# Six of eight merge_b column tiles moved into the attention stage, and the gate weights' loads moved to GpSimd's queue

## The chip, the cores and the metric

The kernel runs on one core of a Trainium2 chip. The metric is device time in microseconds: from the first to the last instruction of the program, with what lies around it. Several executions of the same kernel are taken, and the median is what counts. Beside them one execution was taken with the hardware profiler; all rows below are from that one.

## The reference, cut to what matters

Two blocks of a network run one after the other on 512 tokens of width 1024 in float32. The part that is changed is the end of the first block. `h` is the normalised input, `proj = h @ w_in`, and `merge` is the last 2048 columns of it:

```
m_a, m_b = jnp.split(merge, 2, axis=-1)
y = (jax.nn.sigmoid(m_a) * y_a + jax.nn.sigmoid(m_b) * y_b) @ w_out[l]
x = x + gate[:, None, :] * rms_norm(y, g_post[l])
```

`y_a` and `y_b` are the outputs of two attentions (compressed, selected and windowed heads; sliding-window heads with sinks), each multiplied by `silu(z)` and by its own output matrix. `gate` is a third of `c @ w_ada + b_ada`, so it needs the last 1024 columns of `w_ada` and the vector `c`, but not `h`. The second block (a short convolution mixer and an mLSTM mixer) is not touched.

## The kernel before, in words

All activations lie transposed: a tile has 128 of the 1024 columns on its partitions and the 512 tokens along the free dimension. Float32 products are made of three fast matmuls: both operands are split into a high and a low part (`mm3`, line 481), and `proj` (line 489) adds up eight such triples, 24 matmuls of 512 columns, for one column tile.

**Weights.** All weights are cut into units of 128 x 1024 and used in one fixed order, the list `units` (lines 445 to 474). `Weights` (line 372) has SP load a unit into one of three staging tiles; ScalarE casts the high part `whi`, VectorE subtracts to get the low part `wlo`, into one of three pairs of parts. `W.get()` gives the next unit and starts splits and loads ahead.

**Order.** Every engine call is noted in a `Plan` (line 191) with a duration, a latency and a priority, which is its place in program order. `flush` (line 315) runs a list scheduler over the operations noted since the last flush and emits them: on each engine, of the operations that are ready by its own clock, the one with the smallest priority number. What it emits is each engine's fixed order on the chip. While `plan.prio` is `FILL` (1e6) an operation is taken only when nothing else of its engine is ready. A load issued by GpSimd is priced at 1.0 us for the issue, one issued by SP at 0.05 us (line 207), and either one's data at 345 GB/s (line 357).

**The attention stage** (lines 854 to 1037). Its filling work are sixteen column tiles (lines 886 to 895): eight tiles of `zt`, the `z` gates with silu applied, and eight tiles tanh(m_a / 2), kept in `ma`, a view of `x1`. They go through PSUM banks 6 and 7 in turn. The attention itself is a list of 32 steps: four blocks of 128 queries in the order 1, 2, 3, 0 (`ORDER`), in each two groups of heads and four kinds (`KINDS`). `scores` makes the scores (banks 0 and 1), VectorE adds distances and takes the minimum, ScalarE the exponentials, GpSimd scales the rows; `pv_step` transposes them (banks 2 and 3) and multiplies them with the values (banks 4 and 5). At the end of a group the result is multiplied into the columns of this query block in `zt`; after the second group these columns are split into a high part (ScalarE) and a low part (GpSimd) in `QS` (lines 1030 to 1032). From then on these columns of `zt` are not read any more.

**The merge stage** (lines 1058 to 1103) takes column tiles in four pairs. For each pair there are 48 matmuls on `QS` with a unit of `woa` and one of `wob` (`pab`, four tiles), and 48 on `h` with two units of `wmb`, whose tanh is kept in `tb`. Then VectorE and ScalarE form `(1 + ma) * y_a + (1 + tb) * y_b` and split it into `Th` and `Tl`. Also in each pair `gate_cols` (line 1063) loads 1 MB of `wada` into the only buffer `ada2` and multiplies it by `c` on VectorE, nine operations into `mg`; `gate_mm` sums over the partitions with four tiny matmuls. The loads go through SP's queue, between the loads of the units. `y` (line 1108) then takes the product with `w_out`, in a tile of its own.

**Pools.** A tile pool closes at the end of its phase, and what comes into its memory later waits for all of it.

Of the kernel before, what the change touches and what calls it, by code (L numbers as in the profile page):

```python
# [10 lines left out]
F32 = mybir.dt.float32  # L11
F32R = mybir.dt.float32r
AF = mybir.ActivationFunctionType
OP = mybir.AluOpType
PSUM = bass.MemoryType.PSUM

S = 512
D = 1024
KT = 8
# [6 lines left out]
ORDER = (1, 2, 3, 0)  # L26
KINDS = "swcb"
FILL = 1e6
HALF = T // 2


# [399 lines left out]
def trunk(ctx, tc, a, out):  # L431
    nc = tc.nc
    plan = Plan(nc)
    V, A, G, PE, SP = plan.dve, plan.act, plan.pool, plan.pe, plan.sp

    def pool(stack, name, space=None):
        return Pool(stack.enter_context(tc.tile_pool(name=name, bufs=1, **({"space": space} if space else {}))))

    @contextmanager
    def phase():  # L440
        with ExitStack() as stack:
            yield stack
            plan.flush()
# [3 lines left out]
    def add(name, n, w=1024):  # L447
        for i in (range(n) if isinstance(n, int) else n):
            units.append((a[name][i], w))
# [3 lines left out]
    for i in range(4):  # L453
        add("wm", [i])
        add("wc1", [2 * i, 2 * i + 1])
    add("wm", range(4, 23))
    for p in range(4):
        add("woa", [p])
        add("wob", [p])
        add("wmb", [2 * p, 2 * p + 1])  # L460
    add("wout", 8)
    add("wout", 8)
    for f in range(16):
# [14 lines left out]
    bank = Banks(pool(ctx, "psum", PSUM))  # L478
    W = Weights(plan, wpool, units, 3, 3)
# [6 lines left out]
    def kview(w, kt):  # L486
        return [t.rearrange("p (k c) -> p k c", k=kt) for t in w]

    def proj(ps, w, u, kt=KT, c=slice(0, 128)):

        for k in range(kt):
            mm3(ps, (w[0][:, k, c], w[1][:, k, c]), (u[0][:, k], u[1][:, k]), k == 0, k == kt - 1)
# [83 lines left out]
    hh, hl = uh[:, :, META:], ul[:, :, META:]  # L576
# [58 lines left out]
    with phase() as sx:  # L635
        sp = pool(sx, "sp")
# [56 lines left out]
        for h in (slice(0, 256), slice(256, 512)):  # L693
# [8 lines left out]
            if h.start:  # L702
                m = ada_mac(0)
# [10 lines left out]
        for k in range(KT):  # L714
# [3 lines left out]
            if k + 2 < KT:  # L718
                G.tensor_tensor(x1[:, k + 2, META:], x1[:, k + 2, META:], rbc, op=OP.mult)
                m = ada_mac(k + 2)  # L720
# [12 lines left out]
        among = (2, 3, 4, 5, 0, 1)  # L733
# [6 lines left out]
        t = big(F32)  # L740
# [3 lines left out]
        for q in range(4):  # L744
            wh, wl = kview([t[:, :816] for t in W.get()], 2)
            for t in range(4):
                for kk in range(2):
                    k = 2 * q + kk
# [102 lines left out]


    ma = x1[:, :, META:]
    with phase() as sx:
        sp = pool(sx, "sp2")
        zt = sp.tile([128, 8, S], F32, name="zt")
        B = sp.tile([128, 128 + S], F32, name="B")
        slp = sp.tile([128, 2, 8], F32, name="slp")
        base3 = sp.tile([128, 4, 32], F32, name="base3")
# [27 lines left out]
        for m in range(16):  # L887
            ps = bank(among=(6, 7))
# [102 lines left out]
        steps = []  # L991
# [6 lines left out]
        def pv_step(st, sc):  # L998
            i, g, t, first, last, both = st
            P, k0, nk = sc  # L1000
            if first:
                acc[t == "b"] = bank(among=(4, 5))
            o = acc[t == "b"]
            nj = (nk + 127) // 128
            n = min(nk, 128)
            prev = None
            for jj in range(nj + 1):
                cur = trans(P, jj * 128, n) if jj < nj else None
                if prev is not None:
                    jb = jj - 1  # L1010
                    if t == "c":
                        PE.matmul(o, vcs[:, g], prev[0][:96], start=False, stop=last)
                    else:
                        w = vv[:, k0 // 128 + jb, "swb".index(t), 2 * g:2 * g + 2].rearrange("p a d -> p (a d)")
                        for e in range(2):
                            PE.matmul(o, w, prev[e], start=first and jb == 0 and not e,
                                      stop=last and jb == nj - 1 and e == 1)
                prev = cur
            if last:
                p0 = 4 if t == "b" else 0  # L1020
                qb = slice(i * 128, i * 128 + 128)
                s = slice(64 * g, 64 * g + 64)
                out_g = zt[:, p0:p0 + 4, qb]

                av = sp.tile([128, S], F32, name="av", tag="P", bufs=10)
                A.copy(av[s], o[64 - 64 * g:128 - 64 * g])
                V.tensor_tensor(av[s], av[s], o[s], op=OP.add)
                V.tensor_tensor(out_g[s], av[s].rearrange("p (j q) -> p j q", j=4), out_g[s], op=OP.mult)
                if both:
                    hi = QS[:, p0:p0 + 4, 0, qb]  # L1030
                    A.copy(hi, out_g)
                    G.tensor_tensor(QS[:, p0:p0 + 4, 1, qb], out_g, hi.bitcast(F32), op=OP.subtract)

        for st in steps:
            pv_step(st, scores(*st[:3]))
        W.ahead = 2
    plan.flush()
    kvx.close()
# [19 lines left out]
    with phase() as sx:  # L1058
        sp = pool(sx, "sp3")
# [2 lines left out]

        def gate_cols(i):
            t = sp.tile([128, KT, 256], F32, name="ada2", tag="ada2", bufs=1)
            SP.dma_start(t, a["wada"][8 + i].rearrange("p (k c) -> p k c", k=KT))
            m = [sp.tile([128, 256], F32, name=f"mg{e}", tag=f"mg{e}", bufs=2) for e in range(2)]
            for e in range(2):
                V.tensor_scalar(m[e], t[:, e], vec[:, V_C + e:V_C + e + 1], 0.0, op0=OP.mult, op1=OP.add)
            for k in range(2, KT):
                V.scalar_tensor_tensor(m[k % 2], t[:, k], vec[:, V_C + k:V_C + k + 1], m[k % 2], op0=OP.mult, op1=OP.add)  # L1070
            V.tensor_tensor(m[0], m[0], m[1], op=OP.add)
            return m[0]
# [9 lines left out]
        for p in range(4):  # L1082
            pab = []
            for q0 in (0, 4):
                w = kview(W.get(), 4)
                for e in range(2):
                    ps = bank()
                    proj(ps, w, (QS[:, q0:q0 + 4, 0], QS[:, q0:q0 + 4, 1]), 4, slice(e * 128, e * 128 + 128))
                    pab.append(ps)
            m = gate_cols(p)  # L1090
            for e in range(2):
                pm = bank()
                proj(pm, kview(W.get(), KT), (hh, hl))
                mi = 2 * p + e
                tb = sp.tile([128, S], F32, name="tb", tag="tb", bufs=2)
                ua = sp.tile([128, S], F32, name="ua", tag="ua", bufs=2)
                A.activation(tb, pm, AF.Tanh, scale=0.5)
                V.scalar_tensor_tensor(ua, ma[:, mi], 1.0, pab[e], op0=OP.add, op1=OP.mult)
                V.scalar_tensor_tensor(tb, tb, 1.0, pab[2 + e], op0=OP.add, op1=OP.mult)
                V.tensor_tensor(ua, ua, tb, op=OP.add)  # L1100
                A.activation(Th[:, mi], ua, AF.Copy, scale=0.5)
                V.scalar_tensor_tensor(Tl[:, mi], ua, 0.5, Th[:, mi].bitcast(F32), op0=OP.mult, op1=OP.subtract)
            gate_mm(p, m)
# [1 line left out]
            for k in range(0, KT, 4):  # L1105
                SP.dma_start(x1[:, k:k + 4, META + h:META + h + 256], a["xT"][h // 256, :, k:k + 4])
        SP.dma_start(x1[:, :, :META], a["metaT"].rearrange("(k p) t -> p k t", p=128))
        y = sp.tile([128, KT, S], F32, name="y")

        def wout_half(hf, between):  # L1110
            rs = RS[hf]
# [67 lines left out]
                proj(conv_ps[q][e], conv_w[q], (uh[:, :, HS[e]], ul[:, :, HS[e]]))  # L1179
        W.split_to(W.used + 1)  # L1180


    with phase() as sx:
        sp = pool(sx, "sp4")
# [583 lines left out]
```

## Time and profile before

| | us |
|---|---|
| median of 3 runs | 1512.63 |
| lowest and highest run | 1509.63, 1514.08 |
| the profiled execution: its own time | 1511.26 |
| its span, first to last instruction | 1509.2 |

In the rows further below, PE is TensorE's matmuls and PEld its weight loads, DVE is VectorE, ACT ScalarE, POOL GpSimd and SP the sync engine; a name like SPq or DVEq is that engine's queue of instructions that do not count as busy. Times are microseconds from the start of the span, or nanoseconds where a row gives the mean of one instruction. A matmul's duration in a row overlaps with that of the next: what one costs is read from the distance between two starts. PEclk is the granted clock of TensorE in a stretch, 1.00 being 2.4 GHz. Names after an arrow are what an instruction or a wait was waiting for. Since nearly all recorded operations have the line of the helper that emits them (L254), the tile names tell them apart: `uh` and `ul` are the parts of `h`, `qs` those of the gated attention, `whi` and `wlo` those of a weight unit, `mg` and `ada` the gate product and its weights.

### The profile page before, as it was taken

What the parts mean: (1) busy time and instruction counts of PE and PEld (TensorE: products, weight loads), DVE (VectorE), ACT (ScalarE), POOL (GpSimd) and SP (SyncE); (2) the same over time, 40 slices, a digit from 0 to 9 for tenths busy, and PEclk for the clock granted to TensorE, in tenths of its full rate; (3) what the DMA queues carried; (4) which work ended last, traced back from release to release, by engine and by line L of the source; (5) the groups of instructions that cost most, each with busy time, mean ns of one, the idle gap of its engine ahead of it and who ended that gap; (6) DMA issues with size and microseconds to landing.
All of it is one profiled execution on the core that took longest, in us unless ns stands there. A gap on an engine that the chain in (4) does not pass through costs nothing.

```text
span 1509.2 us, 22556 instructions
## 1 busy us (share of the span) xinstructions
PE 1463.2 (97%) x8965; PEld 1300.1 (86%) x8965; DVE 880.3 (58%) x1710; ACT 606.4 (40%) x1103; POOL 248.2 (16%) x292
## 2 busy tenths in 40 slices
PE   5999999988999899999999999999999999999997
PEld 5787888856889899999999999988888888887886
DVE  7976758776558754454544545755534635453465
ACT  3475757772247422122212122554333333433333
POOL 3210323440002210011001001302002101100201
PEclk8999999989999999999999999999999999999998
DMA  6544121005445232222222222221222222222221
GB/s 232 181 130 149 58 83 43 15 1 183 154 137 171 71 98 85 98 85 98 85 89 94 91 93 79 97 84 55 89 81 84 70 98 71 70 98 83 72 70 56
DMA packets 44121, 142.60 MB, mean 94 GB/s; under 512 B 5745, under 2 KB 12145, under 8 KB 42609
## 3 DMA queue, kind: packets, MB, share of 16 engines
q1 hardware_dynamic: 44016, 141.17, 28.3%
q8 instruction: 70, 1.15, 0.3%
q14 instruction: 35, 0.28, 0.1%
HBM read 139.06 MB, written 2.10 MB: 94 GB/s over the span
## 4 chain that ended last, share of the span: by engine, by line
PE 74%; DVE 2%; DMA 0%; issue 0%; ACT 0%; DVEq 0%; ACTq 0%
PE bank L254 74%; DVE ul L254 0%; DVE y L254 0%; DVE wlo L254 0%; DMA ada<-in_wada 0%; DVE so L254 0%; DVE num L254 0%; DVE x L254 0%; DVE mg L254 0%; DVE ss L254 0%; DVE nss L254 0%; DVEq L1764 0%; ACT Dm L254 0%; DVE tb L254 0%; DVE rb L254 0%
## 5 line engine op out<-in xcount | busy, mean ns | idle before, releaser
L254 PE MATMUL bank<-ul,whi 128*128 128x264 f32 (+1 forms) x1784 | 570.8, 324 | 2.7 <-DVE ul L254 2.5
L254 PE MATMUL bank<-uh,whi 128*128 128x264 f32 (+1 forms) x1784 | 570.6, 325 | 2.2 <-ACT uh L254 2.2
L254 PE MATMUL bank<-uh,wlo 128*128 128x264 f32 (+1 forms) x1768 | 565.9, 324 | 0.0
L254 ACT CAST whi<-wst 128x1024 fp32r<-128x1024 f32 (+2 forms) x236 | 244.6, 1038 | 621.2 <-PE bank L254 452.1
L254 DVE TENSOR_TENSOR wlo<-wst,whi 128x1024 fp32r<-128x1024 f32 (+1 forms) x227 | 279.3, 1232 | 193.8 <-ACT whi L254 192.4
L254 PEld LDWEIGHTS bank<-ul,whi 128*128 128x128 f32 x1784 | 335.8, 188 | 28.9 <-DVE ul L254 4.0
L254 PEld LDWEIGHTS bank<-uh,whi 128*128 128x128 f32 x1784 | 335.4, 189 | 28.6 <-ACT uh L254 3.9
L254 PEld LDWEIGHTS bank<-uh,wlo 128*128 128x128 f32 x1768 | 333.4, 189 | 24.8 <-DVE wlo L254 0.4
L254 DVE TENSOR_TENSOR zr<-bank,rb 128x264 f32<-128x264 f32 (+1 forms) x64 | 35.8, 559 | 118.9 <-PE bank L254 118.9
L254 DVE TENSOR_TENSOR x<-x,bank 128x264 f32<-128x264 f32 (+2 forms) x102 | 49.9, 496 | 68.9 <-PE bank L254 67.4
L254 POOL TENSOR_TENSOR yv<-yv,rb 128x528 f32<-128x528 f32 x16 | 22.7, 1419 | 335.1 <-DVE yv L254 316.8
L254 PE MATMUL bank<-gh,wlo 128*128 128x264 f32 x256 | 72.5, 284 | 0.0
L254 PE MATMUL bank<-gl,whi 128*128 128x264 f32 x256 | 72.4, 283 | 0.0
L254 PE MATMUL bank<-gh,whi 128*128 128x264 f32 x256 | 72.3, 284 | 0.0
L254 POOL TENSOR_SCALAR P<-P,sm 128x256 f32<-128x256 f32 (+3 forms) x96 | 49.7, 536 | 84.4 <-DVE sm L254 38.2
L254 PE MATMUL bank<-whi,uh 128*128 128x512 f32 (+1 forms) x160 | 61.7, 386 | 0.3 <-DVE ak L254 0.3
L254 PE MATMUL bank<-wlo,uh 128*128 128x512 f32 (+1 forms) x160 | 61.7, 386 | 0.0
L254 PE MATMUL bank<-whi,ul 128*128 128x512 f32 (+1 forms) x160 | 61.6, 385 | 0.0
L254 ACT ACTIVATE P<-P,nm 128x256 f32<-128x256 f32 (+3 forms) x96 | 50.8, 530 | 7.4 <-DVE nm L254 6.1
L254 PE MATMUL bank<-Gh,whi 128*128 128x512 f32 (+1 forms) x144 | 53.5, 371 | 0.0
L254 PE MATMUL bank<-Gl,whi 128*128 128x512 f32 (+1 forms) x144 | 53.3, 370 | 0.0
L254 PE MATMUL bank<-Gh,wlo 128*128 128x512 f32 (+1 forms) x144 | 53.3, 370 | 0.0
(336 smaller groups left out, 2294.2 us busy)
## 6 DMA issues: line engine op xcount, KB each, us to landing
wst<-in_wci SPq DMA_DIRECT2D x64, 512.0 KB, 3.4
wst<-in_wqkv SPq DMA_DIRECT2D x32, 512.0 KB, 3.4
wst<-in_wzo SPq DMA_DIRECT2D x32, 512.0 KB, 3.4
wst<-in_wm SPq DMA_DIRECT2D x23, 512.0 KB, 3.4
ada<-in_wada SPq DMA_DIRECT2D x11, 1024.0 KB, 5.2
wst<-in_wout SPq DMA_DIRECT2D x16, 512.0 KB, 4.1
wst<-in_wco SPq DMA_DIRECT2D x16, 512.0 KB, 3.5
wst<-in_wmo SPq DMA_DIRECT2D x16, 512.0 KB, 3.4
```

The costliest lines, as they stand in the source:

```text
L254: call(*[v.real() if isinstance(v, View) else v for v in args], **{k: v.real() if isinstance(v, View) else v for k, v in kw.items()})
```

## The change

Three column pairs' `wmb` units (six of eight) come before the merge's units in the list. After each of the first three query blocks (8, 16 and 24 steps) two of these tiles are noted with `FILL` priority, through banks 6 and 7, and their tanh is written into the 4 x 128 columns of `zt` which this query block has freed; `mb` keeps the views. In the merge these six tiles have no matmuls left, and the product reads `mb` in place of `tb`. `zt` lives on through the merge, in a pool on the right side of the memory, and `y` is written over it. The loads of `gate_cols` are issued by GpSimd. All pools get `reuse_waits="tile"`: a new tile waits for the tiles in whose memory it lies, not for their whole pool.

```diff
+N_EARLY = 6
...
-    def pool(stack, name, space=None):
-        return Pool(stack.enter_context(tc.tile_pool(name=name, bufs=1, **({"space": space} if space else {}))))
+    def pool(stack, name, space=None, **kw):
+        return Pool(stack.enter_context(tc.tile_pool(name=name, bufs=1, reuse_waits="tile", **({"space": space} if space else {}), **kw)))
...
     add("wm", range(4, 23))
+    add("wmb", N_EARLY)
     for p in range(4):
         add("woa", [p])
         add("wob", [p])
-        add("wmb", [2 * p, 2 * p + 1])
+        add("wmb", [m for m in (2 * p, 2 * p + 1) if m >= N_EARLY])
...
+    zx = ExitStack()
+    zt = pool(zx, "zp", side="right").tile([128, 8, S], F32, name="zt")
+    mb = []
     with phase() as sx:
         sp = pool(sx, "sp2")
-        zt = sp.tile([128, 8, S], F32, name="zt")
...
-        for st in steps:
+        for n, st in enumerate(steps):
             pv_step(st, scores(*st[:3]))
+            if (n + 1) % 8 == 0 and len(mb) < N_EARLY:
+
+                plan.prio = FILL
+                for e in range(2):
+                    ps = bank(among=(6, 7))
+                    proj(ps, kview(W.get(), KT), (hh, hl))
+                    mb.append(zt[:, 4 * e:4 * e + 4, st[0] * 128:st[0] * 128 + 128])
+                    A.activation(mb[-1], ps.rearrange("p (n c) -> p n c", n=4), AF.Tanh, scale=0.5)
+                plan.prio = 0
         W.ahead = 2
...
-            SP.dma_start(t, a["wada"][8 + i].rearrange("p (k c) -> p k c", k=KT))
+            G.dma_start(t, a["wada"][8 + i].rearrange("p (k c) -> p k c", k=KT))
...
             for e in range(2):
-                pm = bank()
-                proj(pm, kview(W.get(), KT), (hh, hl))
                 mi = 2 * p + e
...
-                A.activation(tb, pm, AF.Tanh, scale=0.5)
+                if mi >= N_EARLY:
+                    pm = bank()
+                    proj(pm, kview(W.get(), KT), (hh, hl))
+                    A.activation(tb, pm, AF.Tanh, scale=0.5)
...
-                V.scalar_tensor_tensor(tb, tb, 1.0, pab[2 + e], op0=OP.add, op1=OP.mult)
+                tbv, gate, o = tb, tb, pab[2 + e]
+                if mi < N_EARLY:
+                    tbv, o = (t.rearrange("p (n c) -> p n c", n=4) for t in (tb, o))
+                    gate = mb[mi]
+                V.scalar_tensor_tensor(tbv, gate, 1.0, o, op0=OP.add, op1=OP.mult)
...
-        y = sp.tile([128, KT, S], F32, name="y")
+        y = zt
...
+    zx.close()
```

## Rows read from the trace of the kernel before

**Rows 1.** The page, part 1: busy us, share of the span, instructions.

```profile
PE 1463.2 (97%) x8965; PEld 1300.1 (86%) x8965; DVE 880.3 (58%) x1710; ACT 606.4 (40%) x1103; POOL 248.2 (16%) x292
```

**Rows 2.** The chain that ended last: start us, us, what.

```profile
344.92 4.92 DMA ada<-in_wada
...
352.06 1.15 DVE wlo L254
...
510.23 984.01 PE bank L254 x6397
```

**Rows 3.** Windows: us, busy us of each engine, granted clock, DMA share, GB/s.

```profile
146.10:303.41 157.31, 155.68 (x819) 129.23 (x818) 117.66 (x370) 108.04 (x287) 50.99 (x97) 1.00 0.15 48
303.41:340.43 37.02, 30.43 (x139) 21.15 (x137) 30.33 (x127) 29.00 (x102) 15.44 (x38) 0.82 0.00 1
340.43:353.25 12.82, 9.04 (x27) 6.41 (x26) 5.46 (x13) 3.80 (x6) 2.96 (x2) 0.73 0.41 129
353.25:437.36 84.11, 84.11 (x374) 69.05 (x375) 49.63 (x83) 23.80 (x30) 0.00 (x0) 1.00 0.49 169
```

**Rows 4.** Timeline of TensorE: start us, us, what; four stretches at full clock.

```profile
301.39 0.60 PE L254 MATMUL bank<-ident,P 128*128 128x128 f32 x4
...
302.06 0.39 PE L254 MATMUL bank<-pl,vv 128*128 128x512 f32 x1
...
308.89 0.28 PE L254 MATMUL bank<-khw,qs 128*128 128x128 f32 x1
309.00 0.28 PE L254 MATMUL bank<-klw,qs 128*128 128x128 f32 x1
...
425.85 0.40 PE L254 MATMUL bank<-uh,whi 128*128 128x512 f32 x1
...
431.44 0.40 PE L254 MATMUL bank<-uh,whi 128*128 128x512 f32 x1
```

**Rows 5.** Groups of TensorE by shape, 303.4 to 353.24: busy us, mean ns, idle before.

```profile
L254 PE MATMUL bank<-ident,P 128*128 128x128 f32 x48 | 11.3, 325 | 1.7 <-POOL P L254 1.6
L254 PE MATMUL bank<-qs,whi 128*128 128x512 f32 x18 | 8.0, 526 | 2.0 <-ACT qs L254 1.5 <-POOL qs L254 0.6
L254 PE MATMUL bank<-pl,vv 128*128 128x512 f32 x14 | 7.5, 538 | 1.8 <-DVE pl L254 1.7
L254 PE MATMUL bank<-ph,vv 128*128 128x512 f32 x13 | 6.9, 531 | 1.3 <-ACT ph L254 0.9
L254 PE MATMUL bank<-qs,wlo 128*128 128x512 f32 x8 | 3.9, 482 | 0.0
L254 PE MATMUL bank<-ident,Pc 128*32 128x128 f32 x12 | 3.2, 370 | 0.0
L254 PE MATMUL bank<-khb,qs 128*128 128x128 f32 x8 | 2.8, 356 | 0.0
...
L254 PE MATMUL bank<-ph,vcs 96*128 96x512 f32 x3 | 1.8, 593 | 0.0
```

**Rows 6.** Groups by shape, 341.5 to 441: busy us, mean ns, idle before.

```profile
L254 DVE TENSOR_TENSOR wlo<-wst,whi 128x1024 fp32r<-128x1024 f32 x18 | 21.9, 1222 | 23.5 <-ACT whi L254 23.5
L254 ACT CAST whi<-wst 128x1024 fp32r<-128x1024 f32 x18 | 18.8, 1048 | 49.1 <-PE bank L254 32.4 <-DMA wst<-in_wmb 8.1 <-DVE wlo L254 4.5
...
L254 DVE SCALAR_TENSOR_TENSOR mg<-ada,vec,mg 128x256 f32<-128x256 f32 x24 | 10.7, 481 | 0.1
L254 DVE TENSOR_TENSOR ua<-ua,tb 128x512 f32<-128x512 f32 x8 | 5.5, 689 | 0.2
...
L254 ACT ACTIVATE tb<-bank 128x512 f32<-128x512 f32 x8 | 4.7, 592 | 0.0
```

**Rows 7.** Timeline of GpSimd: the last low parts written from zt.

```profile
323.31 1.28 POOL L254 TENSOR_TENSOR qs<-zt,qs 128x512 fp32r<-128x512 f32 x1
...
341.94 2.96 POOL L254 TENSOR_TENSOR qs<-zt,qs 128x512 fp32r<-128x512 f32 x2 [5.52 <-ACT qs L254]
```

**Rows 8.** The tile ada: its thirteen loads on SP's queue, from issue to landing.

```profile
DMA to landing us min/median/max: 4.7/5.5/9.9
```

## The prediction

> **What bounds the kernel now.** I read the page first: TensorE is busy for 97% of the span, no other engine for more than 58% [rows 1]. So only two kinds of change can pay: less TensorE work, or fewer gaps between it. This one keeps every matmul and moves six tiles of them. The second view was the chain that ended last [rows 2]. From 510.23 us on it is one piece of TensorE work, 984 us long, so whatever is gained or lost before that point arrives at the end unchanged. Its first pieces are no matmuls: a transfer of gate weights, then VectorE. The third view, the windows [rows 3], says where the gaps are. While the attention has filling work (146.10 to 303.41) TensorE is busy 155.68 of 157.31 us. From 303.41, when the last filling matmul has been issued, to the attention's last matmul at 340.43, it is busy 30.43 of 37.02 us at a mean granted clock of 0.82, that is partly at the lower of its two levels, 1.2 instead of 2.4 GHz. To 353.25 the clock is 0.73 and 9.04 of 12.82 us are busy. From there to 437.36 the merge has no gap at all. The whole prize therefore lies between 303.41 and 353.25, and "busy" understates it, since a matmul at the low clock counts as busy for longer. I price those matmuls at full speed instead.
>
> **Price of that stretch at full speed.** A merge_b tile of 24 matmuls with 512 columns takes 431.44 - 425.85 = 5.59 us, 0.233 us each; a score matmul 0.11 us; four transposes and one 512-column matmul 0.67 us, so 0.44 us for four transposes [rows 4]. The stretch holds 30 matmuls of 512 columns on the values, 26 on qs, 6 x 8 score matmuls (one of the six alike forms is shown), and 48 + 12 transposes [rows 5]. The attention's own part is 30 x 0.233 + 48 x 0.11 + 15 x 0.44 = 18.9 us, the 26 of the merge are 6.1 us. Of 37.02 us the attention leaves 18.1 free; of the next 12.82, 6.7 are free. **Sum: 24.8 us can be won.**
>
> **The six tiles.** They remove 6 x 5.59 = 33.5 us of TensorE work from the merge and put as much into the attention, behind the sixteen tiles that are there (later count, same FILL priority). By the price above about 18.1 us, three tiles, fit into the attention's gaps; the other 15.4 us stand behind its last matmul and cover what TensorE waited for there: the last gated columns (VectorE, ScalarE, then GpSimd) and the low part of the second weights, held up behind the gate weights [rows 2]. 15.4 is more than 6.7, so 8.7 us remain as cover if the attention ends later. It will end a little later: each tile brings a cast of 1.05 and a tanh of 0.59 us on ScalarE and a split of 1.22 us on VectorE [rows 6]. For the three tiles in the gaps that is 4.9 and 3.7 us, against 29.00 and 30.33 us busy of 37.02 [rows 3]: both fit, tightly. For six it would be 9.8 and 7.3, and ScalarE would need 38.8 of 37.02. The planner gives these operations the lowest priority, so the attention's go first; the 8.7 us take the rest. The nearest row for how well filling works is the stretch before, which lost 1.6 of 157 us [rows 3]; the tail has thinner margins, so I take 2 us lost, between 0 and 18.1 (nothing fits).
>
> The destinations cost nothing in time: two tiles go into columns of a query block that is gated and split already. The last of the three blocks is read for the last time at 323.31 + 1.28 us [rows 7], and its tiles are the fifth and sixth, after 340 by the count above. Cover gone, a tanh that waits there would hold ScalarE's queue and with it the exponentials. The output y in zt waits for gates read a merge earlier: nothing. The pools' waits by tile instead of by pool could free a few first instructions of a phase sooner; inside 303 to 353 that is counted already, elsewhere I take 0, between 0 and 2 us.
>
> **The merge that is left.** Three column pairs now have only 48 matmuls, 11.2 us; the fourth keeps 96, 22.4 us. VectorE has per pair two splits (2.4), the gate product (eight operations of at most 0.48: 3.8), eight products of 0.69 (5.5, of which one form is shown) and 0.3 of small ones: 12.0 us, for the fourth 14.4 with its two more splits [rows 6]. VectorE thus becomes as long as TensorE in three pairs. It may fall behind by 8.7 us (TensorE still fills) plus 22.4 - 14.4 = 8.0 in the fourth pair, so three pairs may take it 33.6 + 16.7 = 50 us. Into that goes the wait for the gate weights, one buffer, so that each load starts when the product before is done. GpSimd's queue holds nothing else here (0.00 busy, [rows 3]), and SP's weight loads no longer stand behind a load that waits. The trace has no load issued by GpSimd. The nearest rows are SP's own: issue to landing 4.7 to 9.9 us, median 5.5 [rows 8]. The planner prices it at 1.0 + 3.04 = 4.0 us (lines 207 and 357) and puts the product into VectorE's order accordingly, so VectorE stands for what exceeds 4.0, and splits and gate products stand behind it. At 5.5 three pairs take 3 x 13.5 = 40.5 us, under 50: free. At 9.9 they take 53.7: 4 us lost. I take 2 us for uneven arrival, between 0 and 4.
>
> The Trainium skill, SBUF — State Buffer, section Who interferes with whom, speaks against the move: a DMA issued by GpSimd can starve while VectorE holds the port pair that they share. By the figure in its section on the bandwidth-pool intuition (620 to 3100 ns, five times) the landing would be some 27 us, an estimate, and the merge would lose 55 us. No run of before shows it; whether a slow landing hurts is worked out as a rival below.
>
> **Sum.** 24.8 - 2 - 2 = 20.8 us. The profiled execution took 1511.26 us, 1.4 under the median of the three runs: 1490.5 us against it, **1491.9 us** against the median.
>
> **Rivals.** *A, the gaps stay empty:* splits at the lowest priority come too late on crowded VectorE and ScalarE, and the tiles run behind the attention. Only the 6.7 us of waits go, less 2: 1507.9 us. For it speaks that VectorE is busy 82% of that stretch; against it the 155.68 of 157.31 us, with the same kind of filling and VectorE at 75% [rows 3]. *B, it does less than it says:* filling uses two PSUM banks, and a tile's bank is free only after its tanh. If the write into zt waits for more than its own columns (the last reads of zt begin at 341.94, [rows 7]), only two tiles, 11.2 us, fit into the gaps. 6.9 us more are lost: 1498.8 us. Nothing in the trace excludes that. *C, slower:* the load through GpSimd lands late, VectorE stands in its order, splits come late and TensorE waits. With landing L, three pairs take VectorE 3 x (8 + L) us; the gain of 22.8 us is used up at L = 16.3. At L = 20 it is 84 - 50 = 34 us lost: 1523.8 us. Against it: the longest landing shown is 9.9. *D, no change:* the extra work makes the attention end late by as much as is won: ScalarE and VectorE serve one chain, and 9.8 + 7.3 us in a row, beyond the cover of 8.7, with A's loss, leave about nothing: 1512 us.
>
> **Numbers.** Differences under 0.3%, 4.5 us, can't be told from no change here. The forecast has 0.55 (1486 to 1496: losses up to 6, or none and the boundaries' 2), B 0.16, A 0.12, D 0.08, C 0.09. A lies on the edge of 4.5 us, two thirds of it faster. Faster 0.55 + 0.16 + 0.08 + 0.03 for the upper half of D's spread = 0.82, same 0.09, slower 0.09. The range reaches from the forecast's low end past B to the near side of A: 1486 to 1505.
>
> **What would show it.** Filling matmuls (uh, ul against weights) after the attention's sixteen tiles, about three before its last matmul; granted clock near 1.00 all through that stretch; no TensorE wait for qs or for the second low part; the merge about 34 us shorter; VectorE's waits for ada of some 1 to 3 us each and no TensorE wait behind them; the first attention stretch and all after the merge as they were. Wrong: a clock of 0.8 in the tail (A or B), a landing over 16 us (C), an attention that ends over 9 us later (D).

## The result and the profile after

Taken together in the same comparison, the changed kernel has a median of 1490.6 us (four runs, 1488.94 to 1492.32), the kernel before 1513.36 us (1509.63 to 1516.5). The ratio is 0.9856, 95% interval 0.9839 to 0.9873: the change makes the kernel faster, by 1.3 to 1.6%, 22.8 us by the medians. The profiled execution took 1492.32 us with a span of 1490.3 us; that of before had a span of 1509.2, so the two profiles differ by 18.9 us.

The page of the changed kernel, part 1 (busy time, share of the span, instructions), answers to [rows 1]:

```profile
PE 1453.2 (98%) x8965; PEld 1296.9 (87%) x8965; DVE 881.8 (59%) x1710; ACT 605.7 (41%) x1103; POOL 251.5 (17%) x296
```

The number of matmuls is the same, 8965. What changed is their order, their idle time and their clock, and GpSimd has four more instructions, the loads.

The windows of the changed kernel, with the columns of [rows 3]: the attention to the end of its sixteenth old tile (its 384 filling matmuls, counted in the trace), the rest of the attention to its last matmul, from there to the first matmul of the merge, and the merge to the first matmul of the product with `w_out`:

```profile
147.36:306.04 158.68, 157.15 (x818) 130.08 (x818) 117.73 (x369) 108.11 (x284) 48.72 (x89) 0.99 0.16 54
306.04:349.82 43.78, 42.22 (x233) 33.74 (x232) 37.97 (x136) 35.66 (x114) 22.16 (x47) 1.00 0.16 50
349.82:361.63 11.81, 11.81 (x52) 9.58 (x51) 2.62 (x6) 3.25 (x5) 2.85 (x3) 1.00 0.43 138
361.63:418.14 56.51, 56.51 (x257) 46.74 (x255) 44.66 (x82) 16.99 (x21) 1.60 (x3) 1.00 0.57 196
```

The second row stands for 303.41 to 340.43 in [rows 3], where TensorE was busy 30.43 of 37.02 us at a clock of 0.82. Now it is busy 42.22 of 43.78 at 1.00. The third and fourth rows have no gap at all. VectorE is busy 44.66 of the 56.51 us of the merge; the prediction counted 3 x 12.0 + 14.4 = 50.4, some of which (the first splits) lies before.

The first row is not what it was: the same work takes 158.68 us, where it took 157.31 in [rows 3], and the clock is 0.99 and not 1.00. All of that lies in one place, where the granted clock falls for a moment:

```profile
260.00:275.00 15.00, 14.01 (x68) 11.55 (x67) 11.95 (x33) 11.54 (x27) 6.26 (x9) 0.89 0.11 37
```

The change is not the cause by itself. Six of the fourteen profiles have this fall, all with four or six tiles moved. But the first profile with four tiles has it (0.89) and the second, of the same program, does not (1.00), though just before it TensorE waits the same 0.7 and 0.3 us for VectorE in both. Nor have it the two runs that differ from the changed kernel only in the queue or in the pools' waits. With the fall the stretch takes 158.6 to 158.7 us, without it 157.1 to 157.3.

The timeline of TensorE in the changed kernel: the attention's last matmul, the filling right behind it, and the end of the filling.

```profile
349.82 0.40 PE L255 MATMUL bank<-pl,vv 128*128 128x512 f32 x1
350.06 0.40 PE L255 MATMUL bank<-ul,whi 128*128 128x512 f32 x1
...
361.40 0.39 PE L255 MATMUL bank<-uh,wlo 128*128 128x512 f32 x1
361.63 0.63 PE L255 MATMUL bank<-qs,whi 128*128 128x512 f32 x2
```

From 350.06 to 361.63 there are 11.57 us of filling, 2.07 tiles at 5.59 us each [rows 4]. So 3.93 of the six tiles ran inside the attention, and the rest covered the wait for the gated columns.

All that TensorE waited for from 147 to 420 us in the changed kernel (total, times, longest):

```profile
PE bank L255 <- DVE Pc L255: 1.2, 3, 0.7
PE bank L255 <- DVE sm L255: 0.9, 1, 0.9
PE bank L255 <- DVE pl L255: 0.6, 1, 0.6
PE bank L255 <- POOL P L255: 0.2, 1, 0.2
```

No wait for `qs` is left, and none for a low part, where [rows 2, 5] had both.

**The account.** The table gives stretches of the two spans, each between two matmuls that can be found in both traces.

| stretch, us | before | after | difference |
|---|---|---|---|
| span start to the attention's first matmul | 146.1 | 147.4 | +1.3 |
| to the attention's last matmul | 193.8 | 202.4 | +8.6 |
| to the first matmul with `w_out` | 97.4 | 68.3 | -29.1 |
| to the next block's first matmul on its gates (`gh`) | 174.8 | 176.1 | +1.3 |
| to the end | 897.0 | 896.0 | -1.0 |

The two middle rows give 20.5 us, where the prediction had 20.8. 3.93 tiles are 22.0 us of TensorE work. The attention took them in and became 8.6 longer. Of this about 1.4 is the fall of the clock, which lies before the gaps; behind the sixteenth old tile it became 7.3 longer (43.8 against 193.8 - 157.3 = 36.5), so 22.0 - 7.3 = 14.7 us of its gaps were filled. The stretch behind lost 22.0 of work and 7.1 of waits and low clock. The first row of the table is no effect of the change: over the fourteen profiles of this case it lies between 143.3 and 147.5 us, whatever the kernel.

### The profile page after: what moved, and what is told of

The parts are those of the page before. It is cut to its first block, busy times and chain, and to the rows that moved or that the text cites. A ratio compares the mean times of both kernels' runs of the same rounds, so it can differ in the third digit from the quotient of the medians.

```text
span 1490.3 us, 22552 instructions
## 1 busy us (share of the span) xinstructions
PE 1453.2 (98%) x8965; PEld 1296.9 (87%) x8965; DVE 881.8 (59%) x1710; ACT 605.7 (41%) x1103; POOL 251.5 (17%) x296
## 3 DMA queue, kind: packets, MB, share of 16 engines
q1 hardware_dynamic: 43440, 136.98, 27.7%
## 4 chain that ended last, share of the span: by engine, by line
PE 91%; DVE 6%; ACT 1%; DMA 1%; issue 0%; POOL 0%; SPq 0%; DVEq 0%; POOLq 0%; ACTq 0%
PE bank L255 91%; DVE mac L255 2%; DVE wlo L255 1%; DMA x<-in_xT 0%; DVE zt L255 0%; DVE ul L255 0%; DMA wst<-in_wm 0%; DVE P L255 0%; POOL P L255 0%; ACT whi L255 0%; ACT P L255 0%; DVE pl L255 0%; SPq L255 0%; DVE ak L255 0%; DVE so L255 0%
## 5 line engine op out<-in xcount | busy, mean ns | idle before, releaser
L255 PE MATMUL bank<-Gl,whi 128*128 128x512 f32 (+1 forms) x144 | 53.3, 370 | 0.0
L255 PE MATMUL bank<-Gh,wlo 128*128 128x512 f32 (+1 forms) x144 | 53.3, 370 | 0.0
```

The costliest lines, as they stand in the source:

```text
L255: call(*[v.real() if isinstance(v, View) else v for v in args], **{k: v.real() if isinstance(v, View) else v for k, v in kw.items()})
```

## The experiments

The first four runs change the number of moved tiles or the queue of the gate loads.

**No tile moved.**

```diff
-N_EARLY = 6
+N_EARLY = 0
```

> N_EARLY = 0: no merge_b tile is moved; zt's place, the gate loads through GpSimd's queue and the waits by tile stay. Theory (the gain is TensorE's idle time in the attention's tail, filled by moved tiles): 1510 to 1514 us, nearly as before, at most some 2 us for the splits no longer held up behind the gate weights. Rival 1 (a good part comes from the loads or from the waits by tile): 1500 us or less.

Measured: 1508.66 us, ratio 0.9965 (0.9951 to 0.998). It is 1.3 us below what was expected, and far from the rival. By the medians, what is left of the change without its tiles is worth some 4 us (5 by the ratio), and the tiles the other 18.

**Two tiles.**

```diff
-N_EARLY = 6
+N_EARLY = 2
```

> N_EARLY = 2: two tiles moved, 2 x 5.59 = 11.2 us of filling. Theory: the tail has 24.8 us to fill, so both tiles pay in full: 1500 to 1503 us. Rival 2 (every moved tile pays a sixth of the gain, 3.7 us): 1505 to 1507.

Measured: 1498.49 us, ratio 0.9904 (0.9881 to 0.9927). Both tiles pay in full, as the theory has it; the time is 1.5 us below its range, which did not count the some 4 us that the run before won without tiles. The attention (first to last matmul) is 194.6 us long, against 193.8 before: 11.2 us of work went in for 0.8 us of time. What TensorE waited for from 300 to 460 us in this run shows that the gaps behind the attention, the waits for `qs`, are still there:

```profile
PE bank L255 <- ACT ph L255: 1.8, 2, 1.5
PE bank L255 <- ACT qs L255: 1.5, 1, 1.5
PE bank L255 <- POOL qs L255: 1.1, 1, 1.1
```

**Four tiles.**

```diff
-N_EARLY = 6
+N_EARLY = 4
```

> N_EARLY = 4: 22.4 us of filling against 24.8 us of room. Theory: nearly all is won with four tiles; 1490 to 1494 us, as with six or up to 3 us above. Rival 2 (a sixth each): 1497 to 1500.

Measured: 1488.36 us, ratio 0.984 (0.9808 to 0.9873), below the expectation and at least as fast as six. All four tiles lie inside, but for two matmuls. The windows of this run, its attention behind the sixteenth old tile and its merge:

```profile
304.81:348.25 43.44, 42.00 (x234) 33.77 (x233) 36.74 (x135) 34.73 (x113) 21.21 (x47) 1.00 0.14 39
...
348.90:416.60 67.70, 67.70 (x306) 55.80 (x304) 48.24 (x89) 21.23 (x27) 3.58 (x5) 1.00 0.56 194
```

The merge begins 0.7 us after the attention's last matmul and has no gap, without the 11.57 us of filling that six tiles put there. The attention ends 202.1 us after its start, about as late as with six (202.4), but both have the fall of the clock at 260 to 275 us. Without it, in the later profile of this same program, it takes 200.5 us, and with six tiles 200.9. So the four tiles fill 22.4 - (200.5 - 193.8) = 15.7 us of gaps, 5.3 more than the first two alone (11.2 - 0.8 = 10.4). What the third and fourth bring besides is behind the attention: the waits for `qs` are gone, and the stretch from the last matmul to `w_out` falls from 83.8 us with two tiles to 68.3, which is 4.3 more than their own 11.2. The fifth and sixth fill nothing: with six the same stretch takes 68.3 too.

**Six tiles, the gate weights on the sync engine's queue as before.**

```diff
-            G.dma_start(t, a["wada"][8 + i].rearrange("p (k c) -> p k c", k=KT))
+            SP.dma_start(t, a["wada"][8 + i].rearrange("p (k c) -> p k c", k=KT))
```

> Six tiles moved, the gate loads back on SP's queue, waits by tile. Theory: the tiles alone make the gain and VectorE's slack in the merge covers a load from either queue: 1489 to 1493 us, as the change. Rival 3 (GpSimd's queue is needed: on SP the gate loads wait for the product and hold up the units' loads, now with half the TensorE work per pair): 1496 us or more, with TensorE waits in the merge.

Measured: 1490.77 us, ratio 0.9852 (0.9826 to 0.9878). The rival falls: with six tiles GpSimd's queue gives nothing. The first load leaves at 347.10 us, 0.4 after the attention's last matmul, and VectorE waits for the gates 2.2 us in two waits, as the rows for VectorE say:

```profile
DVE mg L255 <- DMA ada<-in_wada: 2.2, 2, 1.6
```

**Six tiles, waits for whole pools.**

```diff
-... bufs=1, reuse_waits="tile", **({"space": space} if space else {}), **kw)))
+... bufs=1, **({"space": space} if space else {}), **kw)))
```

> The changed kernel with waits for whole pools, as before, and all else kept. The prediction priced the waits by tile at 0 (0 to 2 us). Theory: they are worth about 1 us at the end of the program (last stage 14 to 15 us after the last matmul instead of 13.9), and at the start of the merge nothing, because filling matmuls run there: 1490 to 1493 us. Rival: without them the new pool on the right side and what lies in the attention's memory wait for everything of the phase before, at several boundaries: 1496 us or more, with TensorE idle at 361 to 365 us.

Measured: 1488.93 us, ratio 0.9851 (0.9836 to 0.9866). The time is 1.1 us below the expected range; its profile is one of those without the fall of the clock in the attention. Nothing is lost at the start of the merge, as expected. The microsecond at the end was not lost either (896.1 us from `gh` to the end, as in the changed kernel), so the waits by tile do not give it. With six tiles they are worth nothing that can be measured.

**Late gate loads.** This is the prediction's rival C, tried by making it true: each load is issued three times in a row, priced as one.

```diff
-            G.dma_start(t, a["wada"][8 + i].rearrange("p (k c) -> p k c", k=KT))
+            src = a["wada"][8 + i].rearrange("p (k c) -> p k c", k=KT)
+            plan.add("POOL", lambda: [nc.gpsimd.dma_start(t.real(), src) for _ in range(3)], [], [t], 1.0, 2.0, None, t.arr.size * 4)
```

> The changed kernel, but each of the four loads of gate weights is issued three times in a row by GpSimd, so that the data land late while the planner still prices one load. This tries the prediction's rival C. Theory: the landing takes 16 to 20 us instead of 5 to 7.5; VectorE stands in its fixed order for it, the splits behind it come late and TensorE waits. By the prediction's sum, three pairs take VectorE 3 x (8 + 18) = 78 us, of which 50 are free: some 28 us lost, 1510 to 1522 us. Rival: the loads run so far ahead of their product that the transfer stays hidden: under 1497 us and no TensorE wait for a low part.

Measured: 1521.19 us, ratio 1.0066 (1.005 to 1.0083), in the theory's range and slower than the kernel before. The timeline of GpSimd in this run shows the three issues of the first load (each waits until the one before has landed) and the first issue of each later one:

```profile
353.99 0.74 POOL L1079 DMA_DIRECT2D ada<-in_wada  x1
360.48 0.54 POOL L1079 DMA_DIRECT2D ada<-in_wada  x1 [5.74 <-DMA ada<-in_wada]
365.78 0.53 POOL L1079 DMA_DIRECT2D ada<-in_wada  x1 [4.76 <-DMA ada<-in_wada]
376.34 0.53 POOL L1079 DMA_DIRECT2D ada<-in_wada  x1 [10.03 <-DVE mg L255]
...
397.65 0.53 POOL L1079 DMA_DIRECT2D ada<-in_wada  x1 [8.31 <-DVE mg L255]
...
420.51 0.53 POOL L1079 DMA_DIRECT2D ada<-in_wada  x1 [7.91 <-DVE mg L255]
```

and the timeline of VectorE the start of the gate product with its wait:

```profile
370.78 0.62 DVE L255 TENSOR_SCALAR mg<-ada,vec 128x256 f32<-128x256 f32 x2 [17.85 <-DMA ada<-in_wada]
...
393.76 0.62 DVE L255 TENSOR_SCALAR mg<-ada,vec 128x256 f32<-128x256 f32 x2 [8.65 <-DMA ada<-in_wada]
...
417.23 0.62 DVE L255 TENSOR_SCALAR mg<-ada,vec 128x256 f32<-128x256 f32 x2 [12.27 <-DMA ada<-in_wada]
```

From the first issue to the product it is 16.8 us, then 17.4, and for the third load 19.6: 17.9 on average. TensorE's waits from 360 to 450 us show the rest of the chain:

```profile
PE bank L255 <- DVE mg L255: 14.5, 2, 8.7
PE bank L255 <- DVE wlo L255: 7.6, 1, 7.6
```

By the prediction's sum three pairs take VectorE 3 x (8 + 17.9) = 77.7 us, 50 are free, 27.7 are lost. Measured, between medians of two comparisons: 1521.2 - 1490.6 = 30.6. In the traces the merge, from its first matmul on `qs` to the first with `w_out`, takes 86.6 us against 56.5, so 30.1 more.

**Twice instead of three times**, with `range(2)`.

> The changed kernel with each gate load issued twice in a row by GpSimd: a landing of 11 to 13 us, between the 5 to 7.5 of one load and the 16 to 20 of three. It tries where lateness begins to cost. Prediction's sum: three pairs take VectorE 3 x (8 + 11.5) = 58.5 us, of which 50 are free: 8 us lost, 1496 to 1501 us. Rival: what is free is smaller, because VectorE's order is fixed and a late product holds up the very next split; then each pair loses the whole excess of its period over TensorE's 11.2 us, 3 x 4.5 = 13 us or more: 1503 us and above.

Measured: 1505.74 us, ratio 0.9948 (0.9932 to 0.9964): in the rival's range. Again the timelines, GpSimd's first issue of each load:

```profile
351.32 0.74 POOL L1079 DMA_DIRECT2D ada<-in_wada  x1
...
368.40 0.53 POOL L1079 DMA_DIRECT2D ada<-in_wada  x1 [10.11 <-DVE mg L255]
...
385.60 0.53 POOL L1079 DMA_DIRECT2D ada<-in_wada  x1 [8.97 <-DVE mg L255]
...
404.57 0.53 POOL L1079 DMA_DIRECT2D ada<-in_wada  x1 [13.05 <-DVE mg L255]
```

and VectorE's products:

```profile
362.85 0.62 DVE L255 TENSOR_SCALAR mg<-ada,vec 128x256 f32<-128x256 f32 x2 [12.60 <-DMA ada<-in_wada]
381.71 0.62 DVE L255 TENSOR_SCALAR mg<-ada,vec 128x256 f32<-128x256 f32 x2 [5.34 <-DMA ada<-in_wada]
401.29 0.62 DVE L255 TENSOR_SCALAR mg<-ada,vec 128x256 f32<-128x256 f32 x2 [8.38 <-DMA ada<-in_wada]
```

The landings were 11.5, 13.3 and 15.7 us, 13.5 on average, not the 11.5 assumed. With 13.5 the prediction's sum gives 3 x 21.5 - 50 = 14.5 us; measured are 1505.7 - 1490.6 = 15.1, and in the traces the merge takes 73.2 us, 16.7 more than in the changed kernel.

The total of the sum thus comes near in both runs, but its terms are not what the timelines show. From the first issue of one load to that of the next it is 17.1, 17.2 and 19.0 us with two loads and 22.4, 21.3 and 22.9 with three: both times the landing and then 5.6, 3.9 and 3.3 us, 4.2 on average, where the sum has 8. With one load it is 12.5, 12.1 and 11.8 us (GpSimd's timeline in the next section), about VectorE's own work of a pair, which the prediction put at 12.0. So the rest of that work runs while the load is under way, and a pair takes the larger of some 12 us and the landing plus 4.2. The three pairs take 36.4 us with one load, 53.3 with two and 66.5 with three; what goes beyond 36.4, 16.9 and 30.1 us, is what the merge became longer (16.7 and 30.1). So the rival holds in kind too: what is free is smaller than 50 us, and each pair loses its whole excess. The two misses of the sum nearly cancel in the threshold: 36.4 / 3 - 4.2 = 7.9 us of landing, where the sum had 50 / 3 - 8 = 8.7. No run lies at it.

**What the change is worth without tiles and without GpSimd.** Two runs divide the 4 us of the first run. The first has N_EARLY = 0 and the sync engine's loads, and keeps the waits by tile and the place of the z tile:

> No tile moved, the gate weights on the sync engine's queue as before; only the waits by tile and the place of the z tile are left of the change. The run with no tile moved and GpSimd's queue was some 4 us faster than the kernel before. Theory: the waits by tile give that, about 1 us at the end of the program and 2 to 3 at the start of the merge: 1507 to 1510 us. Rival: GpSimd's queue gives it, since the sync engine's weight loads no longer stand behind a load that waits: 1511 to 1514 us here.

Measured: 1508.53 us, ratio 0.9982 (0.9972 to 0.9992), in the theory's range, so GpSimd's queue is not what gives it: from the attention's first matmul to `w_out` it takes 289.0 us here and 289.1 in the run with that queue, against 291.2 before. The second has waits for whole pools as well:

> No tile moved, the sync engine's queue for the gate weights, waits for whole pools: of the change only the place of the z tile (a pool of its own on the right side, y written over it) is left. It divides the 3 us that the run with the waits by tile had won. Theory: the first gate load leaves at 340 us there and at 345 before, because it no longer waits for the whole pool of the attention; so without waits by tile it leaves at 345 again, and the time is 1511 to 1514 us, the merge 95 us long. Rival: it is the place of the z tile, and the load leaves at 340 us here too: 1507 to 1510 us.

Measured: 1509.22 us, ratio 0.9978 (0.9968 to 0.9989). By the time the theory fell and its rival came in: the gain of some 3 us is there without the waits by tile, so it comes from the place of the z tile. The rival's mark, a load at 340 us, came in only by half. The queue of the sync engine shows when the first gate load leaves, first in the run with the z tile's place alone:

```profile
343.58 0.33 SPq L255 DMA_DIRECT2D ada<-in_wada  x1
```

then in the run that also has waits by tile:

```profile
340.19 0.33 SPq L255 DMA_DIRECT2D ada<-in_wada  x1
```

Counted from the attention's last matmul (339.94, 340.92 and 339.37 us), the load leaves 4.98 us later in the kernel before, 2.66 with the z tile elsewhere and 0.82 with waits by tile. In the kernel before it left when GpSimd had read the last of `zt` (341.94 + 2.96 = 344.90, [rows 7]), because `zt` lay in the attention's pool and the load's buffer waits for that pool. The merge is 95.5, 93.4 and 92.8 us long, and the wait for a low part at its start (1.7 us before) is gone in both. So 2.1 us come from the place. The 0.6 of the waits is half lost again in a longer attention (194.2 against 193.9 us), and the two ratios do not tell the runs apart. The rest is at the end of the program (896.2 us in both, against 897.0), which no part of the change explains, as told below.

**Which number of tiles is best.** Two runs in one comparison: four tiles with GpSimd's queue, and the changed kernel again.

> Four tiles moved and GpSimd's queue, once more, beside the changed kernel in the same comparison. Theory: the stage after the product with w_out takes 173 us with four tiles and 176 with six, and nothing else differs: 2 to 3 us under the changed kernel. Rival: the difference seen before lay in the runs: within 1 us of it.

> The changed kernel itself, for the comparison with four tiles: 1490 to 1492 us by its earlier runs; the one with four 2 to 3 us less (theory), or the same within 1 us (rival).

Measured: 1487.63 us with four (1484.75 to 1488.09; ratio to before 0.9825, 0.9808 to 0.9843), 1490.38 with six (1489.88 to 1491.99; 0.9849, 0.9833 to 0.9866). The two intervals overlap, the four runs of each do not: in this comparison four tiles are some 2.7 us faster. In the earlier run with four tiles they spread wider, from 1485.61 to 1491.69 us. The time is the theory's, but its reason is not: in these two profiles the stage behind `w_out` takes 174.8 and 176.1 us, half of the difference, and from the attention's first matmul to `w_out` it is 268.9 with four and 270.7 with six. Most of the latter is the fall of the clock in the attention, which this profile with four tiles does not have:

```profile
260.00:275.00 15.00, 14.00 (x82) 11.72 (x81) 12.56 (x35) 13.57 (x36) 8.21 (x11) 1.00 0.11 37
```

The profiles with the fall take 270.4 us with four tiles and 270.7 or 270.8 with six, those without it 268.9 with four and 269.2 or 269.3 with six (in the runs with the sync engine's queue and with pool waits). So up to `w_out` four tiles are 0.3 to 0.4 us faster, which is next to nothing. The rest lies behind `w_out`, and there too it goes with the clock (last section). That four tiles are better is thus shown as a time in this comparison; the filling has little part in it, and most of it goes with the granted clock.

**Four tiles with the sync engine's loads.**

> Four tiles moved instead of six, and the gate weights on the sync engine's queue: the two runs that were each at least as fast as the changed kernel, together. Theory: both parts are worth nothing or a little, and four tiles are all that fit into the gaps: 1485 to 1489 us. Rival: with only four tiles nothing covers the start of the merge, and the gate loads between the weights' loads make TensorE wait there again: 1491 to 1495 us.

Measured: 1491.54 us, ratio 0.9868 (0.9854 to 0.9882), in the rival's range. TensorE's waits from 330 to 480 us begin with the one that [rows 2] had, a low part behind the gate weights:

```profile
PE bank L255 <- DVE wlo L255: 2.0, 1, 2.0
```

So GpSimd's queue and the cover of two more tiles do the same thing: either one hides the first gate load, and without both some 2 us come back (272.7 us from the attention's first matmul to `w_out`, against 270.4 with the queue and the same fall of the clock). Four tiles with GpSimd's queue are the best version found.

## Why the prediction was right, and where its terms were off

The forecast was 1491.9 us, and the measured 1490.6 lies in its own narrow range. Its main marks came in: clock 1.00 in the tail, no wait for `qs` or a low part, and the merge that is left is gapless. It is 39.0 us shorter (95.5 to 56.5), where the mark had about 34, since the waits at its start went too. Of the rest, the waits for the gates came otherwise (below), and the first attention stretch, which was to stay as it was, became 1.4 us longer with the fall of the clock. The terms under the sum were less exact than their total: that 20.5 us came out where 20.8 were forecast is in part luck, since two misses cancel.

- **"About three" tiles in the gaps** were 3.93, because the attention ended 8.6 us later and not "a little". The step said that 18.1 us are free and 2 are lost, so 16.1 are won; 14.7 were, and 1.4 went to the fall of the clock before them. TensorE still idles 43.78 - 42.22 = 1.6 us there, no more than was allowed for. But the price by units was too small: less 94 filling matmuls of 0.233 us, 21.9 in all, TensorE is busy 42.2 - 21.9 = 20.3 us for an attention priced at 18.9.
- **"8.7 us remain as cover if the attention ends later"**: it ended 8.6 later, and 7.1 in the two runs with six tiles and no fall of the clock. That is within the cover and just short of rival D's mark ("over 9 us later"). It was not D's mechanism. Apart from the 1.4, the attention ends late because TensorE is full (96% busy at clock 1.00, with 1.5 us of waits for VectorE), not because VectorE (37.97 of 43.78 us) or ScalarE (35.66) are; work that fills TensorE is not lost.
- **Two microseconds lost to uneven arrival in the merge** were none. Behind the attention's last matmul 7.1 us were won, where the step had 6.7 - 2 = 4.7. This miss and the first one cancel.
- **The gate loads.** The landing was taken at 5.5, with waits of 1 to 3 us for each. GpSimd's timeline in the changed kernel:

```profile
354.75 0.74 POOL L255 DMA_DIRECT2D ada<-in_wada  x1
367.25 0.54 POOL L255 DMA_DIRECT2D ada<-in_wada  x1 [11.76 <-DVE mg L255]
379.32 0.53 POOL L255 DMA_DIRECT2D ada<-in_wada  x1 [11.53 <-DVE mg L255]
391.13 0.53 POOL L255 DMA_DIRECT2D ada<-in_wada  x1 [11.28 <-DVE mg L255]
```

and VectorE's waits for them from 345 to 420 us:

```profile
DVE mg L255 <- DMA ada<-in_wada: 8.0, 1, 8.0
```

  VectorE waited once, for 8.0 us and under the filling, and for the other three not at all. The first landing took 361.68 - 354.75 = 6.9 us; over the four, issue to landing is 5.1 to 7.5 us, median 6.2, against 4.8 to 7.1, median 5.2, for the sync engine's loads in the run with its queue. That difference does not last: over the twelve profiles in which each load is issued once, the median is 5.3 us for GpSimd's 28 loads and 5.8 for the sync engine's 20. The rule of the Trainium skill, SBUF — State Buffer, section Who interferes with whom, that a DMA issued by GpSimd can starve beside VectorE, would have meant 27 us by the prediction's estimate, which scales the landing by five. The trace shows nothing like it, but it does not try the rule: that section of the Trainium skill ties the starving to VectorE's 2-port modes, which it gives for copies, casts and tensor_scalar. Nor does the page of the Trainium skill behind that estimate have such a load grow in proportion: it waits until the VectorE instruction ends. During the first of the four landings VectorE stood still, and during the others, where it was busy for 4.4 to 6.7 us, all that it ran was tensor_tensor and scalar_tensor_tensor.

  The sum for the merge was mis-built, too. The planner's price is not 4.0 us: line 207 also gives each load 2.0 us of latency, and line 192 adds 0.2, both on top of the 3.04 us of data, while GpSimd's 1.0 is not in the way of the data. So the product is placed 5.2 us or more behind the issue, and it came 8.1 to 8.5 us behind, which is why three landings of 5.1 to 7.5 us cost nothing. That a late landing costs about what rival C said is shown by the two runs with doubled and tripled loads. It was a right mechanism with a condition that did not hold: the first three landings were 6.9, 7.5 and 5.1 us, 6.5 on average, 1.4 under the 7.9 of the timelines.
- **"The pools' waits by tile ... I take 0"** held with six tiles. But the place of the z tile, for which the prediction had no term, is worth some 2 to 3 us when no tile covers the merge's start. About 2 of these are among the 6.7 us that were counted as waits anyway.
- **Not foreseen:** the stage behind `w_out` became 1.3 us longer, and the end of the program 1.0 shorter. The first is told below. For the second the runs give no cause: the stretch from `gh` to the end takes 897.0 us in the kernel before and in the run with three loads, and 896.0 to 896.4 in every other, with and without each part of the change. It stays open.

Rivals A and B are out: the gaps did fill, and the write into `zt` held nothing up, since nearly four tiles ran before the last read of `zt`.

## What to carry to other kernels

Price what lies idle at the full clock, then ask how much of it the filling can reach without delaying the chain that it fills: here the first two tiles cost the chain 0.8 us, the next two 5.9 (in the profile without the fall of the clock), and the last two bought nothing. So try the number of moved pieces, not only the move. Where a load's buffer is freed by an engine that then has to use it, its price is a threshold, not a sum: landings of 5.1 to 7.5 us cost nothing, since the engine's other work runs meanwhile, and beyond some 8 us each microsecond was paid three times, once per pair (4.4 us more of landing made the merge 13.4 longer). And look at what else a tile's place in a pool holds up: one tile moved out of a pool let a load in another pool leave 2.3 us earlier. Before a microsecond between two kernels is explained, compare two profiles of one of them: here the clock alone moved a stretch by 1.4 us between two executions of the same program.

## What the runs showed that was not expected

The clock of TensorE falls in a stage that the change does not touch. Windows of the first 20 us after the last matmul with `w_out`, for the kernel before and the one with four tiles of the first 30, first of the kernel before:

```profile
483.00:493.00 10.00, 9.17 (x71) 8.34 (x69) 9.24 (x19) 4.39 (x11) 5.20 (x4) 1.00 0.49 157
493.00:503.00 10.00, 9.04 (x71) 8.55 (x71) 9.41 (x20) 5.65 (x15) 4.10 (x5) 1.00 0.01 2
503.00:513.00 10.00, 7.06 (x51) 6.41 (x49) 9.33 (x25) 5.26 (x10) 2.26 (x3) 0.95 0.16 52
```

then of the changed kernel:

```profile
463.80:473.80 10.00, 5.08 (x28) 4.54 (x27) 9.26 (x19) 4.38 (x11) 5.07 (x4) 0.78 0.49 157
473.80:483.80 10.00, 10.00 (x62) 9.71 (x62) 7.40 (x16) 4.82 (x13) 2.87 (x4) 0.71 0.00 0
```

and of the second run with four tiles:

```profile
460.60:470.60 10.00, 8.54 (x65) 7.67 (x64) 9.37 (x19) 4.38 (x11) 5.30 (x4) 1.00 0.54 157
470.60:480.60 10.00, 9.64 (x75) 9.15 (x76) 9.29 (x19) 5.65 (x15) 3.99 (x5) 1.00 0.01 2
480.60:490.60 10.00, 7.05 (x46) 6.41 (x45) 9.33 (x25) 5.26 (x10) 2.39 (x3) 0.88 0.16 52
```

The first profile with four tiles, the same program, has the last of these stretches without a fall:

```profile
482.20:492.20 10.00, 7.06 (x55) 6.42 (x54) 9.33 (x25) 5.26 (x10) 2.31 (x3) 1.00 0.16 52
```

Six tiles leave the same work in another order: TensorE's idle time of 4.9 us lies in the first ten, the granted clock falls there and averages 0.71 in the next ten, where TensorE is busy all the time with fewer matmuls (62 against 71). Its waits there, in the changed kernel from 455 to 515 us:

```profile
PE bank L255 <- DVE ss L255: 2.0, 1, 2.0
PE bank L255 <- DVE wlo L255: 1.8, 1, 1.8
PE bank L255 <- ACT whi L255: 1.1, 1, 1.1
```

In the other order TensorE idles 2.9 us in the third ten instead. There the clock falls as well, for a shorter time (0.95 in the kernel before, and 0.88 in the ten behind), but not in every profile.

From the first matmul with `w_out` to the first on `gh` it takes 176.1 us in five of the six profiles with six tiles (175.0 with three loads of the gates), 174.7 to 174.9 with none or two. With four it is 174.8 us in the profile with a fall and 173.3 and 173.6 in the two without. So the 1.3 us that the changed kernel loses here to the kernel before go with a longer fall of the clock. The order alone does not decide, for the same program took 173.3 and 174.8. An order found by a planner that does not know of the clock can thus give back a microsecond a hundred microseconds later. That the order brings the long fall is likely, since all six profiles with six tiles fall in the first twenty and none of the others does, but it was not tried by itself, nor what in the planner's choice makes that order.

Two smaller things: a load that is issued again into the same buffer leaves only when the one before has landed, 4.8 to 5.7 us of waiting for GpSimd in the first group of three issues; and so a second load of 1 MB adds its own time from issue to landing (5.0 to 10.3 us for the eight loads of the run with two).
